# Layer norms by token tiles, a mixer that begins with dv, and the residual's affine part on VectorE

## The chip, the cores and the metric

The kernel runs on one core of a Trainium2 chip. A core has five engines with a queue each: TensorE (PE; matrix products into PSUM, and transposes), VectorE (DVE), ScalarE (ACT), GpSimd (POOL) and SyncE (SP), which issues the loads and stores. Each engine executes its own instructions in the order in which they are written; between engines, semaphores order what depends on each other. The metric is the device time of one execution in microseconds.

## The reference

One transformer block over 256 tokens of width 2048, in fp32. `ada` is a vector of shifts, scales and gates made from a condition `c`; it modulates each part, and after each part stands a layer norm over the residual:

```python
y = swiglu_ffn(x * (1 + scale[0]) + shift[0], w_ffn_in[0], w_ffn_out[0])
x = layer_norm(ALPHA * x + 0.5 * gate[0] * y, ln_g[0], ln_b[0])
y = hybrid_mixer(x * (1 + scale[1]) + shift[1], w_in, ...)
x = layer_norm(ALPHA * x + gate[1] * y, ln_g[1], ln_b[1])
y = swiglu_ffn(x * (1 + scale[2]) + shift[2], w_ffn_in[1], w_ffn_out[1])
x = layer_norm(ALPHA * x + 0.5 * gate[2] * y, ln_g[2], ln_b[2])
```

`swiglu_ffn` is `(silu(g) * u) @ w_out` with a hidden width of 5632. `hybrid_mixer` projects its input to the queries, keys and values of a differential attention (dq, dk, dv; 8 heads), to those of a gated delta rule (nq, nk, nv, with a short convolution over time, an output gate nz, and the gates nb and na), and to two merge gates (ga, gb); the two branches are merged and multiplied by `w_out`.

## The kernel before

**Precision.** Every product is made of three (`mm3`, lines 145 to 150): an operand is split into a high part of the type fp32r (ScalarE, a copy) and a low part (the operand minus its high part), and hi x hi, hi x lo and lo x hi are added up in PSUM. So each weight chunk, 128 x 1024, is loaded by SP (`raw`), split by ScalarE (`hi`) and by VectorE, or by GpSimd where `pool_lo` says so (`lo`), and then used by TensorE (`_split`, lines 177 to 198). Six `raw` buffers and four `hi`/`lo` buffers let loads and splits run ahead of the products; `weights` (line 219) hands out the next chunk of a plan that is written once for the whole kernel (lines 1524 to 1563), after issuing the splits of the next three chunks and the loads of six.

**Order.** The schedule is written out by hand. Products are emitted one after the other, and after each the kernel lets its threads (generators for the elementwise work) emit instructions when an estimated time has come. This estimate decides only the order in the queues; on the chip the engines wait for each other by semaphores.

**The two kinds of product.** `_wstat` keeps a weight tile stationary and streams 256 columns of the activations `h` (which is kept transposed, as row blocks f = 0 to 15 of 128 features by 256 tokens). `_xstat` keeps an activation tile of 128 tokens stationary and streams 512 columns of the weights; its result has tokens on the partitions. There are two token tiles, t = 0 and 1. `_y_blocks` (line 715) makes y by `_xstat` in four blocks of 512 columns and adds it to the residual `x` (`_residual`, line 700: `res` = y times the gate, the add into `x`, statistics for the layer norm). In the last block, the last two weight chunks (`TAIL`) are used tile by tile and half by half, so that t = 0 is complete first; `finish.step` (stages 0 to 3) is called at these points.

**The passage from part to part** is `_Next` (lines 549 to 629). Stage 0 sets `pool_lo` to 1 for the last block. Stage 1 (after tile 0's residual) takes tile 0's mean and variance and the root; stage 2 (after the first half of tile 1's residual) makes tile 0's factors; stage 3 (after all of it) normalises `x` (tile 0 on ScalarE, tile 1 on VectorE), and `rest` transposes `x` on TensorE into PSUM (`lnt`, 32 transposes), two row blocks with both tiles at a time, and `_h_tile` (line 516) makes of each the next part's `h`: `hf` = A times it plus B on VectorE, `h_hi` on ScalarE from `hf`, `h_lo` on GpSimd. A and B hold the layer norm's weights and the modulation. The first products (`pre`) follow as `h` becomes ready: for the mixer the keys and queries of heads 0 and 1 by `_wstat`, 192 instructions of 256 columns; for the last FFN the first block by `_xstat`, 96 of 512 columns (`wide`). In the middle of it, x is written to DRAM (`xd`) for the next residual.

**The residual's affine part.** `_load_x` (line 676) loads `x` again during a later stage, and as the stored x is normalised but not scaled, multiplies it by `ln_g` and adds `ln_b`: for each quarter of the columns and each tile two GpSimd instructions of 128 x 512, with the rows `rowg` and `rowb` in one buffer each. This happens in the mixer's merge stage and in the last FFN.

**The mixer's order** is `MIXER_JOBS` (line 41): d0, v, d1, a0, d2, a1, d3, a2, a3. A d job projects the keys and queries of two heads of the delta rule, their v, and for d0 also the gates (`_gate_proj`, `_gates`), and starts a thread for the pair (`_delta_pair`, "pair 0" and so on); v makes dv, 1024 columns in two halves; an a job makes nz and two attention heads. Group 0's keys and queries are those made in the passage.

Of the kernel before, what the change touches and what calls it, by code (L numbers as in the profile page):

```python
# [18 lines left out]
S = 256  # L19
# [72 lines left out]
class _Kernel:  # L92
# [84 lines left out]
    def _split(self):  # L177
# [14 lines left out]
        self.A.activation(hi, raw, AF.Copy)  # L192
        eng = self.P if self.pool_lo and i % self.pool_lo == 0 else self.V
        eng.tensor_tensor(lo, raw, hi.bitcast(F32), ALU.subtract)
# [92 lines left out]
def _xprod(k, ps, w, act, kt, j, t, lo, hi, last):  # L287

    act.need(k, kt)
    sl = slice(j * 512 + lo, j * 512 + hi)  # L290
    tk = slice(t * 128, (t + 1) * 128)
    k.mm3(ps[:, lo:hi], (_tile(act[0], kt)[:, tk], _tile(act[1], kt)[:, tk]), (w[0][:, sl], w[1][:, sl]),
          start=(kt == 0), stop=(kt == last))
    k.pump()
# [219 lines left out]
class _Ln:  # L514
# [25 lines left out]
    def norm(self, t, q, eng=None):  # L540
        x = self.k.x[t][:, q * 512:(q + 1) * 512]
        r, b = self.rs[:, t, 0:1], self.rs[:, t, 1:2]
        if t == 0 or eng == "A":
            self.k.A.activation(x, x, AF.Identity, bias=b, scale=r)
        else:
            self.k.V.tensor_scalar(x, x, r, b, ALU.mult, ALU.add)


class _Next:


    def __init__(self, k, idx, prep, wide):
        self.k, self.idx, self.prep, self.wide = k, idx, prep, wide

    def step(self, stage, ada, ln):
        k = self.k
        if stage == 0:
            k.pool_lo = 1
            self.A = None
        elif stage == 1:  # L560
            ln.root(0)
        elif stage == 2:
            ln.factors(0)
        else:
            ln.norm(0, 0)
            ln.norm(0, 1)
            ln.root(1)
            return self.rest(ln)
        if self.A is None and (ada.thread.done or stage == 2):
            k.wait(lambda: ada.thread.done)  # L570
            self.A, self.B = self.prep(ada)

    def rest(self, ln):
        k, A, B = self.k, self.A, self.B
        h = _new_h(k)
        x, lnp = k.x, k.lnp
        k.xd = k.drp.tile([128, 2, D], F32, tag="xd", name=f"xd{self.idx}")

        def turn(ps, g, t):
            for j in range(2):  # L580
                f = 2 * g + j
                k.tr(ps[:, j, t * 128:(t + 1) * 128], x[t][:, f * 128:(f + 1) * 128])

        def bank(g):
            ps = k.pss.tile([128, 2, 256], F32, tag="sm", name=f"lnt{k.uid()}")
            turn(ps, g, 0)
            return ps

        ln.norm(0, 2)
        ln.norm(0, 3)  # L590
        pss = [bank(g) for g in range(3)]
        ln.factors(1)
        ln.norm(1, 0)
        k.pool_lo = 0
        def run():
            for g in range(8):
                ps = pss.pop(0)
                turn(ps, g, 1)
                for i in range(2):
                    f = 2 * g + i  # L600
                    _h_tile(k, lnp, h, f, ps[:, i, :], A[:, f:f + 1], B[:, f:f + 1])
                if g in (0, 2, 4):
                    ln.norm(1, 1 + g // 2)
                h.ready = 2 * g + 2
                h.when[2 * g] = h.when[2 * g + 1] = k.chain
                yield 0.0
                if g < 5:
                    pss.append(bank(g + 3))
            for t in range(2):
                k.nc.sync.dma_start(k.xd[:, t, :], x[t])  # L610

        th = k.spawn(run())
        th.step()
        if self.wide:
            pre = [k.bank([128, 512], "pre") for _ in range(2)]
            for c in range(8):
                w = k.weights()
                for j in range(2):
                    for t in range(2):
                        _xprod(k, pre[t], w, h, 2 * c + j, j, t, 0, 512, KT - 1)  # L620
            k.wait(lambda: th.done)
            return h, pre
        acts = [h, h]
        pre = [k.bank([128, 2, S], "pre") for _ in range(2)]
        for c in range(4):
            for ps in pre:
                _products(k, ps, k.weights(), 4 * c, 4, acts, c == 0, c == 3)
        k.wait(lambda: th.done)
# [47 lines left out]
def _load_x(k, a, pool, rows, tags, idx, delay, pace):  # L676
# [11 lines left out]
    for q in range(4 if idx is not None else 0):  # L688
# [4 lines left out]
        yield 8.0  # L693
        for t in range(2):
            k.P.tensor_tensor(x[t][:, sl], x[t][:, sl], g, ALU.mult)
            k.P.tensor_tensor(x[t][:, sl], x[t][:, sl], b, ALU.add)
# [18 lines left out]
def _y_blocks(k, nchunk, act, ada, sub, first, ln, finish, tail):  # L715

    for n in range(4):
# [5 lines left out]
        def done(t, ps, lo, hi, n=n, last=last):  # L723
# [3 lines left out]
            _residual(k, n, t, ps, lo, hi, ada.dst[(sub, 2)], first, ln.st if ln else None)  # L727
# [5 lines left out]
        if last:  # L733
            k.wait(ready)
            ln.table()
            finish.step(0, ada, ln)
        _xstat(k, nchunk, act, done, tail if last else 0)
# [607 lines left out]
def _mixer(k, a, h, pre, mk_ada, finish):  # L1345
    nc, tc = k.nc, k.tc
    acts = [h, h]
    with ExitStack() as mctx:
# [5 lines left out]
        with tc.tile_pool(name="dp", bufs=1) as dp:  # L1354
# [10 lines left out]
            def delta_jobs(g):  # L1365
# [3 lines left out]
                for hd in (2 * g, 2 * g + 1):  # L1369
                    ps = _wstat(k, 4, acts) if g else pre[hd]  # L1370
                    t = dp.tile([128, 2, S], F32, tag="kq2", name=f"kq2_{hd}", bufs=4)
                    conv(t, ps, (8 + hd, hd), 1 if g else 2 - hd)
                    kq2.append(t)
                if g == 0:
                    before.append(k.spawn(_gates(k, _gate_proj(k, h))))
                ps = _wstat(k, 4, acts)
# [14 lines left out]

            for part, g in MIXER_JOBS:
# [4 lines left out]
                else:  # L1397
                    for n in range(2):
                        def done(t, ps, lo, hi, n=n):
                            yield 0.3  # L1400
                            k.A.activation(dv[:, t, n * 512:(n + 1) * 512], ps, AF.Copy)
# [363 lines left out]
```

## Time and profile before

| | us |
|---|---|
| three timed runs | 2392.42, 2395.93, 2392.65 (median 2392.65) |
| the profiled execution | 2389.68 |
| its span, from the first to the last instruction | 2387.9 |
| mean granted clock of TensorE, as a share of full speed | 0.984 |
| first passage (to the mixer) | 786.6 to 824.4 |
| mixer's jobs | to about 1270 |
| merge stage, with the residual's affine part | 1340 to 1420 |
| second passage (to the last FFN) | 1624.05 to 1659.4 |

Times in the profile are microseconds from the start of the span. TensorE's matrix products (PE) and its weight loads (PEld) have rows of their own; a busy PE can still be at half clock, which the granted clock shows. In a timeline, rows of equal instructions that follow each other are merged (x2), and the brackets hold the engine's idle time before the row and what ended it.

### The profile page before, as it was taken

To read this page: it belongs to the slowest core of one execution; us is meant where nothing else is said; L and a number is where in the kernel's file an instruction comes from. 1 tells how busy PE (TensorE), PEld (TensorE's weight loads), DVE (VectorE), ACT (ScalarE), POOL (GpSimd) and SP (SyncE) were. 2 spreads that over 40 slices of the span, in tenths; PEclk is the share of its full clock that TensorE was granted. 3 is DMA by queue.
4 is the path that set the end of the run, shared out by engine and by line. 5 is a ranking of instruction groups with operands and counts; after the bars stand their busy time and mean duration, and the time that the engine had idled before them with its cause. 6 is when DMAs were issued, how large, how long until landed. Compare 5 with 4: busy or idle time off the path is not lost.

```text
span 2387.9 us, 36796 instructions
## 1 busy us (share of the span) xinstructions
PE 2305.5 (97%) x14217; PEld 2071.9 (87%) x14217; DVE 1707.0 (71%) x2508; ACT 1033.1 (43%) x1390; POOL 329.1 (14%) x218
## 2 busy tenths in 40 slices
PE   6999999999999899999999999999999999999997
PEld 6999997888888889988999999987878888888886
DVE  5667888787775688878887887786787555544556
ACT  4434444434444444454444434444444443444432
POOL 5884000000001310000000220013050000000001
PEclk8999999999999999999999999999999999999999
DMA  9998878899875566454546888876888556655553
GB/s 362 332 327 292 300 250 274 305 339 322 315 267 189 176 204 209 157 173 149 170 162 244 298 296 306 286 282 204 310 302 309 189 192 194 193 187 192 188 187 111
DMA packets 166359, 581.70 MB, mean 244 GB/s; under 512 B 19820, under 2 KB 22812, under 8 KB 165416
## 3 DMA queue, kind: packets, MB, share of 16 engines
q1 hardware_dynamic: 166184, 579.36, 70.7%
q8 instruction: 111, 1.82, 0.3%
q14 instruction: 64, 0.52, 0.1%
HBM read 572.98 MB, written 7.88 MB: 243 GB/s over the span
## 4 chain that ended last, share of the span: by engine, by line
PE 86%; DVE 7%; issue 2%; DMA 1%; POOL 1%; ACT 1%; SPq 0%; DVEq 0%; ACTq 0%; POOLq 0%
PE mx L148 17%; PE mx L147 17%; PE mx L149 17%; PE mm L147 6%; PE mm L148 6%; PE mm L149 6%; PE mms L148 4%; PE mms L149 4%; PE mms L147 4%; DVE lo L88 2%; DVE acc L88 1%; PE UY L153 1%; DVE x L88 1%; ACT hi L88 1%; PE hT L158 1%
## 5 line engine op out<-in xcount | busy, mean ns | idle before, releaser
L88 ACT ACTIVATE hi<-raw 128x1024 fp32r<-128x1024 f32 x769 | 811.6, 1059 | 968.7 <-PE mx L149 669.3
L88 DVE TENSOR_TENSOR lo<-raw,hi 128x1024 fp32r<-128x1024 f32 x690 | 855.7, 1246 | 495.7 <-ACT hi L88 485.4
L147 PE MATMUL mx<-hi,h_hi 128*128 128x512 f32 x992 | 389.7, 393 | 0.0
L149 PE MATMUL mx<-hi,h_lo 128*128 128x512 f32 x992 | 387.2, 390 | 0.0
L148 PE MATMUL mx<-lo,h_hi 128*128 128x512 f32 x992 | 387.0, 390 | 0.0
L147 PE MATMUL mm<-h_hi,hi 128*128 128x256 f32 x1216 | 354.4, 291 | 0.0
L149 PE MATMUL mm<-h_hi,lo 128*128 128x256 f32 x1216 | 346.5, 285 | 3.4 <-DVE lo L88 3.4
L148 PE MATMUL mm<-h_lo,hi 128*128 128x256 f32 x1216 | 346.4, 285 | 0.0
L88 POOL TENSOR_TENSOR lo<-raw,hi 128x1024 fp32r<-128x1024 f32 x79 | 190.2, 2415 | 788.0 <-ACT hi L88 788.0
L147 PE MATMUL mx<-hi,hid 128*128 128x512 f32 (+1 forms) x768 | 285.1, 371 | 1.4 <-ACT hi L88 1.4
L148 PE MATMUL mx<-lo,hid 128*128 128x512 f32 (+1 forms) x768 | 284.7, 371 | 0.8 <-DVE lo L88 0.8
L149 PE MATMUL mx<-hi,hid 128*128 128x512 f32 (+1 forms) x768 | 284.5, 370 | 0.0
L147 PE MATMUL mms<-h_hi,hi 128*128 128x256 f32 x896 | 256.2, 286 | 10.2 <-ACT hi L88 5.9
L148 PE MATMUL mms<-h_lo,hi 128*128 128x256 f32 x896 | 256.2, 286 | 3.7 <-POOL h_lo L88 3.7
L149 PE MATMUL mms<-h_hi,lo 128*128 128x256 f32 x896 | 255.9, 286 | 1.6 <-POOL lo L88 1.6
L149 PEld LDWEIGHTS mm<-h_hi,lo 128*128 128x128 f32 x1216 | 235.2, 193 | 3.9 <-DVE lo L88 3.9
L147 PEld LDWEIGHTS mm<-h_hi,hi 128*128 128x128 f32 x1216 | 235.7, 194 | 1.7 <-issue 1.6
L148 PEld LDWEIGHTS mm<-h_lo,hi 128*128 128x128 f32 x1216 | 235.7, 194 | 0.7 <-issue 0.6
L149 PEld LDWEIGHTS mx<-hi,h_lo 128*128 128x128 f32 x992 | 186.6, 188 | 39.2
L147 PEld LDWEIGHTS mx<-hi,h_hi 128*128 128x128 f32 x992 | 186.7, 188 | 38.2 <-issue 0.2
L148 PEld LDWEIGHTS mx<-lo,h_hi 128*128 128x128 f32 x992 | 186.7, 188 | 38.0 <-issue 0.2
L147 PEld LDWEIGHTS mms<-h_hi,hi 128*128 128x128 f32 x896 | 174.4, 195 | 10.9 <-ACT hi L88 6.1
(304 smaller groups left out, 3236.2 us busy)
## 6 DMA issues: line engine op xcount, KB each, us to landing
raw<-in_w_ffn_in_dram SPq DMA_DIRECT2D x240, 512.0 KB, 4.7
raw<-in_w_ffn_out_dram SPq DMA_DIRECT2D x176, 512.0 KB, 4.1
raw<-in_w_first_dram SPq DMA_DIRECT2D x112, 512.0 KB, 5.0
ar<-in_w_gate_dram SPq DMA_DIRECT2D x96, 512.0 KB, 5.1
ar<-in_w_ada_dram SPq DMA_DIRECT2D x96, 512.0 KB, 5.1
sar<-in_w_ada_dram SPq DMA_DIRECT2D x64, 512.0 KB, 5.0
raw<-in_w_gab_dram SPq DMA_DIRECT2D x64, 512.0 KB, 4.5
raw<-in_w_kq_dram SPq DMA_DIRECT2D x32, 512.0 KB, 3.6
```

The source lines that it names most:

```text
L88: return f(*args, **kw)
L147: mm(ps, lhsT=lhs[0], rhs=rhs[0], start=start, stop=False, skip_group_check=True)
L148: mm(ps, lhsT=lhs[0], rhs=rhs[1], start=False, stop=False, skip_group_check=True)
L149: mm(ps, lhsT=lhs[1], rhs=rhs[0], start=False, stop=stop, skip_group_check=True)
L153: self.nc.tensor.matmul(ps, lhsT=lhsT, rhs=rhs, start=start, stop=stop, skip_group_check=True)
L158: self.nc.tensor.transpose(ps, src, self.ident if ident is None else ident)
```

## The change

- The last block of a part no longer sends the lo halves to GpSimd.
- The layer norm goes by token tile. Stage 1 makes tile 0's factors and normalises it at once, two quarters on ScalarE and two on VectorE. Stage 2 comes after tile 1's last product and before tile 1's residual: eight transposes and the first four row blocks of `h` for tile 0 alone. `h` is made in pieces of 128 x 128 (`tile`): `hf` on VectorE and `h_hi` on ScalarE both from PSUM, `h_lo` on GpSimd.
- The first products take tile 0 alone for the first four weight chunks (eight row blocks), then tile 1 for the same four, then both. In both passages they are `_xstat` products of 512 columns. Two of their chunks are split early into space that is free by then (`HELD`, `room`): the tags of hidden blocks in the first passage, in halves of 512 columns, and those of `ya` in the second.
- For the mixer these first products are the first half of dv in place of group 0's keys and queries, which now follow as in the other groups, after the gates; v makes the second half alone.
- x is written to DRAM after all first products.
- `_load_x` makes the affine part on VectorE, an instruction every 2 us by the estimate (from 8 to 12 us for a quarter).

```diff
-        self.A.activation(hi, raw, AF.Copy)
         eng = self.P if self.pool_lo and i % self.pool_lo == 0 else self.V
-        eng.tensor_tensor(lo, raw, hi.bitcast(F32), ALU.subtract)
+        parts = [(hi, lo, raw)]
+        if isinstance(hi, list):
+            parts = [(hi[j], lo[j], raw[:, j * 512:(j + 1) * 512]) for j in range(2)]
+        for h, l, r in parts:
+            self.A.activation(h, r, AF.Copy)
+            eng.tensor_tensor(l, r, h.bitcast(F32), ALU.subtract)
...
+    HELD = 2
+
+    def __init__(self, k, idx, prep):
+        self.k, self.idx, self.prep = k, idx, prep
+
+    def room(self, n):
+
+        k, j0 = self.k, SIZES[0][1] + 4 * n
+        t = [k.hp.tile([128, 512], F32R, tag=f"hid{j0 + i}", name=f"hold{k.uid()}") for i in range(4)]
+        return t[:2], t[2:]
 
     def step(self, stage, ada, ln):
         k = self.k
         if stage == 0:
-            k.pool_lo = 1
             self.A = None
         elif stage == 1:
             ln.root(0)
-        elif stage == 2:
-            ln.factors(0)
-        else:
-            ln.norm(0, 0)
-            ln.norm(0, 1)
-            ln.root(1)
-            return self.rest(ln)
         if self.A is None and (ada.thread.done or stage == 2):
             k.wait(lambda: ada.thread.done)
             self.A, self.B = self.prep(ada)
+        if stage == 1:
+            ln.factors(0)
+            for q, e in enumerate("AVVA"):
+                ln.norm(0, q, e)
+        elif stage == 2:
+            self.h = _new_h(k)
+            self.ps, self.h.ready = {}, KT
+            self.turn(0, 0)
+            self.turn(0, 1)
+            for f in range(4):
+                self.tile(0, f)
+        elif stage == 3:
+            return self.rest(ln)
+
+    def turn(self, t, g):
+
+        k = self.k
+        ps = self.ps[t, g] = k.pss.tile([128, 4, 128], F32, tag="sm", name=f"lnt{k.uid()}")
+        for j in range(4):
+            f = 4 * g + j
+            k.tr(ps[:, j, :], k.x[t][:, f * 128:(f + 1) * 128])
+
+    def tile(self, t, f):
+
+        k, h = self.k, self.h
+        src, tk = self.ps[t, f // 4][:, f % 4, :], slice(t * 128, (t + 1) * 128)
+        A, B = self.A[:, f:f + 1], self.B[:, f:f + 1]
+        hf = k.lnp.tile([128, 128], F32, tag="hf", name=f"hf{k.uid()}", bufs=4)
+        k.V.tensor_scalar(hf, src, A, B, ALU.mult, ALU.add)
+        k.A.activation(h[0][:, f, tk], src, AF.Identity, bias=B, scale=A)
+        k.P.tensor_tensor(h[1][:, f, tk], hf, h[0][:, f, tk].bitcast(F32), ALU.subtract)
 
     def rest(self, ln):
-        k, A, B = self.k, self.A, self.B
-        h = _new_h(k)
-        x, lnp = k.x, k.lnp
+        k, h = self.k, self.h
+        pre = [k.bank([128, 512], "pre") for _ in range(2)]
+
+        def products(c, w, ts):
+            for j in range(2):
+                for t in ts:
+                    _xprod(k, pre[t], w, h, 2 * c + j, j, t, 0, 512, KT - 1)
+
+        ln.root(1)
+        for f in range(4, 6):
+            self.tile(0, f)
+        ln.factors(1)
+        for q, e in enumerate("AVVA"):
+            ln.norm(1, q, e)
+        for f in range(6, 8):
+            self.tile(0, f)
+        w = [k.weights(), k.weights()]
+        products(0, w[0], (0,))
+        products(1, w[1], (0,))
+        self.turn(0, 2)
+        self.turn(0, 3)
+        w += [k.weights(), k.weights(1)]
+        products(2, w[2], (0,))
+        products(3, w[3], (0,))
+        self.turn(1, 0)
+        self.turn(1, 1)
+        for f in range(8):
+            self.tile(1, f)
+        for f in range(8, 10):
+            self.tile(0, f)
+        for c in range(4):
+            products(c, w[c], (1,))
+            if c == 1:
+                self.turn(1, 2)
+                self.turn(1, 3)
+            if c:
+                for f in (8 + 2 * c, 9 + 2 * c):
+                    self.tile(0, f)
+            if c >= 2:
+                for f in range(4 * c, 4 * c + 4):
+                    self.tile(1, f)
+        for c in range(4, 8):
+            products(c, k.weights(), (0, 1))
         k.xd = k.drp.tile([128, 2, D], F32, tag="xd", name=f"xd{self.idx}")
...
+        for t in range(2):
+            k.nc.sync.dma_start(k.xd[:, t, :], k.x[t])
...
-        yield 8.0
+        yield 4.0
         for t in range(2):
-            k.P.tensor_tensor(x[t][:, sl], x[t][:, sl], g, ALU.mult)
-            k.P.tensor_tensor(x[t][:, sl], x[t][:, sl], b, ALU.add)
+            for v, op in ((g, ALU.mult), (b, ALU.add)):
+                yield 2.0
+                k.V.tensor_tensor(x[t][:, sl], x[t][:, sl], v, op)
...
+        lead, late = last and isinstance(finish, _Next), []
+
+        def done(t, ps, lo, hi, n=n, last=last, lead=lead, late=late):
             while not ready(n):
                 yield 0.5
             yield 0.3
-            _residual(k, n, t, ps, lo, hi, ada.dst[(sub, 2)], first, ln.st if ln else None)
+
+            def residual(ps, lo, hi):
+                _residual(k, n, t, ps, lo, hi, ada.dst[(sub, 2)], first, ln.st if ln else None)
+
+            if lead and t == 1:
+                late.append((ps, lo, hi))
+                if lo:
+                    finish.step(2, ada, ln)
+                    for x in late:
+                        residual(*x)
+                return
+            residual(ps, lo, hi)
             if last and (t, lo) == (0, 256):
                 finish.step(1, ada, ln)
...
+            for i in range(finish.HELD if lead else 0):
+                k.held[k.nu + nchunk + i] = finish.room(i)
...
-                for hd in (2 * g, 2 * g + 1):
-                    ps = _wstat(k, 4, acts) if g else pre[hd]
-                    t = dp.tile([128, 2, S], F32, tag="kq2", name=f"kq2_{hd}", bufs=4)
-                    conv(t, ps, (8 + hd, hd), 1 if g else 2 - hd)
-                    kq2.append(t)
                 if g == 0:
                     before.append(k.spawn(_gates(k, _gate_proj(k, h))))
+                for hd in (2 * g, 2 * g + 1):
+                    ps = _wstat(k, 4, acts)
+                    t = dp.tile([128, 2, S], F32, tag="kq2", name=f"kq2_{hd}", bufs=4)
+                    conv(t, ps, (8 + hd, hd))
+                    kq2.append(t)
...
+            def dv_part(t, ps, n):
+                yield 0.3
+                k.A.activation(dv[:, t, n * 512:(n + 1) * 512], ps, AF.Copy)
+
+            for t in range(2):
+                k.read(dv_part(t, pre[t], 0), 2 - t)
...
+                    _xstat(k, 8, h, lambda t, ps, lo, hi: dv_part(t, ps, 1))
...
+        def room(n):
+            both = mp.tile([128, NH, S], F32R, tag=f"ya{'hl'[n]}", name=f"hold{k.uid()}").rearrange("p a b -> p (a b)")
+            return both[:, 0:1024], both[:, 1024:]
+
+        finish.room = room
         return _y_blocks(k, 8, mg, ada, 1, True, _Ln(k), finish, TAIL)
...
-                        plan += [a["w_kq"][hd, c] for c in range(4) for hd in range(2)]
+                        plan += [a["w_dv"][0, c] for c in range(8)]
                         plan += [a["w_ba"][c] for c in range(2)]
-                    else:
-                        plan += [a["w_kq"][hd, c] for hd in (2 * g, 2 * g + 1) for c in range(4)]
+                    plan += [a["w_kq"][hd, c] for hd in (2 * g, 2 * g + 1) for c in range(4)]
...
-                    plan += [a["w_dv"][n, c] for n in range(2) for c in range(8)]
+                    plan += [a["w_dv"][1, c] for c in range(8)]
```

## Rows read from the trace of the kernel before

**Rows 1.** The page's busy table: us, share of the span, instructions
```profile
PE 2305.5 (97%) x14217; PEld 2071.9 (87%) x14217; DVE 1707.0 (71%) x2508; ACT 1033.1 (43%) x1390; POOL 329.1 (14%) x218
```

**Rows 2.** Two stages, the first products alone (columns as in rows 3)
```profile
786.60:824.40 37.80, 25.91 (x192) 24.22 (x192) 0.00 (x0) 0.00 (x0) 0.91 0.50 178
...
1624.05:1659.40 35.35, 25.73 (x96) 18.49 (x96) 0.00 (x0) 0.00 (x0) 0.86 0.53 187
```

**Rows 3.** Stages: us, busy us (instructions) PE PEld DVE ACT POOL, clock, DMA
```profile
803.90:824.40 20.50, 20.50 (x173) 20.50 (x172) 11.08 (x14) 9.31 (x13) 4.61 (x7) 1.00 0.60 203
...
1641.10:1659.30 18.20, 18.19 (x82) 15.08 (x83) 11.55 (x13) 9.45 (x13) 5.99 (x9) 1.00 0.79 283
...
789.50:793.40 3.90, 2.02 (x9) 0.99 (x9) 2.80 (x9) 2.80 (x6) 0.01 (x1) 0.60 0.00 0
...
1360.00:1370.00 10.00, 10.00 (x86) 10.00 (x85) 8.92 (x8) 4.44 (x5) 6.61 (x5) 1.00 0.67 235
...
1370.00:1380.00 10.00, 7.69 (x65) 7.49 (x63) 9.93 (x8) 2.60 (x3) 7.48 (x4) 1.00 0.96 351
...
1380.00:1390.00 10.00, 8.99 (x47) 8.40 (x48) 8.93 (x9) 4.40 (x6) 6.90 (x4) 0.66 0.77 239
...
1750.00:1760.00 10.00, 8.32 (x36) 6.34 (x34) 9.93 (x8) 4.76 (x7) 6.88 (x5) 1.00 0.76 227
...
1060.00:1080.00 20.00, 16.61 (x129) 16.07 (x128) 11.66 (x32) 10.35 (x29) 2.64 (x4) 0.91 0.32 106
```

**Rows 4.** Timeline of PE: start, us, instruction, idle before and its releaser
```profile
789.48 1.37 PE L158 MATMUL lnt<-ident,x 128*128 128x128 f32 x6 [2.67 <-ACT x L88]
...
793.37 0.58 PE L147 MATMUL pre<-h_hi,hi 128*128 128x256 f32 x1 [1.08 <-ACT h_hi L88]
...
1627.52 1.54 PE L158 MATMUL lnt<-ident,x 128*128 128x128 f32 x6 [3.33 <-ACT x L88]
...
1380.72 0.79 PE L153 MATMUL aps<-acchi,ones 128*128 128x512 f32 x1 [3.03 <-ACT acchi L88]
```

**Rows 5.** Timeline of DVE in the first passage
```profile
782.98 1.97 DVE L88 TENSOR_TENSOR x<-x,res 128x256 f32<-128x256 f32 x1
...
785.76 0.42 DVE L88 TENSOR_TENSOR x<-x,res 128x256 f32<-128x256 f32 x1
...
789.86 0.37 DVE L88 BATCH_NORM_AGGREGATE mv<-st 128x2 f32<-128x48 f32 x1
...
790.99 0.55 DVE L88 TENSOR_SCALAR x<-x,rs 128x512 f32<-128x512 f32 x1
...
794.75 2.52 DVE L88 TENSOR_TENSOR lo<-raw,hi 128x1024 fp32r<-128x1024 f32 x2 [0.98 <-ACT hi L88]
```

**Rows 6.** Timeline of ACT in the first passage
```profile
788.61 1.52 ACT L88 ACTIVATE x<-x,rs 128x512 f32<-128x512 f32 x2 [1.22 <-DVE rs L88]
```

**Rows 7.** Timeline of POOL in the first passage
```profile
798.26 6.05 POOL L88 TENSOR_TENSOR h_lo<-hf,h_hi 128x256 fp32r<-128x256 f32 x8 [3.20 <-ACT h_hi L88]
```

**Rows 8.** Timeline of DVE in the merge stage
```profile
1348.52 1.85 DVE L88 TENSOR_TENSOR lo<-raw,hi 128x1024 fp32r<-128x1024 f32 x1 [0.39 <-ACT hi L88]
...
1350.29 3.48 DVE L88 SCALAR_TENSOR_TENSOR acc<-ar,cs,acc 128x512 f32<-128x512 f32 x2
...
1388.47 3.25 DVE L88 SCALAR_TENSOR_TENSOR acc<-ar,cs,acc 128x512 f32<-128x512 f32 x3
...
1393.91 1.53 DVE L88 SCALAR_TENSOR_TENSOR acc<-ar,cs,acc 128x512 f32<-128x512 f32 x2
...
1415.37 0.68 DVE L88 TENSOR_TENSOR acclo<-acc,acchi 128x512 fp32r<-128x512 f32 x1
```

**Rows 9.** Timeline of SP's queue in the merge stage
```profile
1366.09 0.33 SPq L691 DMA_DIRECT2D rowg<-in_ln_g_dram  x1
```

**Rows 10.** Chain of waits from 915 to 960: start, us, what
```profile
924.44 0.89 PE inter L153 x8
...
953.91 1.08 PE GB L153 x8
```

More of the change, by code (lines that the diff above doesn't have):

```diff
@@ L289, in _xprod @@
     act.need(k, kt)
-    sl = slice(j * 512 + lo, j * 512 + hi)
     tk = slice(t * 128, (t + 1) * 128)
-    k.mm3(ps[:, lo:hi], (_tile(act[0], kt)[:, tk], _tile(act[1], kt)[:, tk]), (w[0][:, sl], w[1][:, sl]),
+    w = [x[j][:, lo:hi] if isinstance(x, list) else x[:, j * 512 + lo:j * 512 + hi] for x in w]
+    k.mm3(ps[:, lo:hi], (_tile(act[0], kt)[:, tk], _tile(act[1], kt)[:, tk]), w,
           start=(kt == 0), stop=(kt == last))
@@ L538, in factors, with norm @@
         k.V.tensor_tensor(rs[:, t, 1:2], rs[:, t, 2:3], rs[:, t, 0:1], ALU.mult)
-    def norm(self, t, q, eng=None):
+    def norm(self, t, q, eng):
         x = self.k.x[t][:, q * 512:(q + 1) * 512]
         r, b = self.rs[:, t, 0:1], self.rs[:, t, 1:2]
-        if t == 0 or eng == "A":
+        if eng == "A":
             self.k.A.activation(x, x, AF.Identity, bias=b, scale=r)
@@ L549 @@
 class _Next:
-    def __init__(self, k, idx, prep, wide):
-        self.k, self.idx, self.prep, self.wide = k, idx, prep, wide
+    HELD = 2
[5 more added lines that the diff above has]
+        return t[:2], t[2:]
     def step(self, stage, ada, ln):
@@ L571, in step @@
             self.A, self.B = self.prep(ada)
-    def rest(self, ln):
-        k, A, B = self.k, self.A, self.B
-        h = _new_h(k)
-        x, lnp = k.x, k.lnp
-        k.xd = k.drp.tile([128, 2, D], F32, tag="xd", name=f"xd{self.idx}")
[L579 to L628, printed above, removed]
@@ L721, in ready @@
             return (sub, 2, n) in ada.ready and k.x is not None
-        def done(t, ps, lo, hi, n=n, last=last):
+        lead, late = last and isinstance(finish, _Next), []
+        def done(t, ps, lo, hi, n=n, last=last, lead=lead, late=late):
             while not ready(n):
@@ L1397, in _mixer @@
                 else:
[L1398 to L1401, printed above, removed]
-                        _xstat(k, 8, h, done)
+                    _xstat(k, 8, h, lambda t, ps, lo, hi: dv_part(t, ps, 1))
             pgs = [_wstat(k, 4, acts) for _ in range(3)]
@@ L1629, in prep1 @@
         return _affine(k, 2, 1, d[(2, 0)], d[(2, 1)])
-    h, pre = _ffn(k, a, h, 0, FFN_ADA, FFN_PACE, start, None, _Next(k, 0, prep0, False), TAIL)
-    h, pre = _mixer(k, a, h, pre, lambda pool: _Ada(k, a, pool, TAIL_ADA, TAIL_PACE), _Next(k, 1, prep1, True))
+    h, pre = _ffn(k, a, h, 0, FFN_ADA, FFN_PACE, start, None, _Next(k, 0, prep0), TAIL)
+    h, pre = _mixer(k, a, h, pre, lambda pool: _Ada(k, a, pool, TAIL_ADA, TAIL_PACE), _Next(k, 1, prep1))
     last = _Last(k, a, out)
```

## The prediction, made before the changed kernel was run

> **What bounds the kernel now.** I read the page's busy table first. TensorE is busy for 97% of the span [rows 1]: the kernel is TensorE's, and a change pays only where TensorE stands still or runs at half clock. So I went to the stages, to find where it does, and then to the timelines of the engines there. The reader is to see four places.
>
> Two are the passages between the parts, where a layer norm stands between the last product of one part and the first of the next. In the first, 786.6 to 824.4, TensorE issues 192 first products of 256 columns [rows 2] and 32 transposes. Its full rate is 173 instructions in 20.5 us, 0.1185 each [rows 3]; 192 products need 22.8 us and the transposes, at that rate, 3.8. The passage lasts 37.8: 11.2 us are lost. In the second, 1624.05 to 1659.4, 96 products of 512 columns at 18.2 / 82 = 0.222 need 21.3, the transposes 3.8, and 35.35 pass: 10.2 lost [rows 2, 3]. TensorE's own rows say where: its first transpose starts at 789.48 after 2.67 us of idling, its first product at 793.37 after a stop for `h_hi`; in the second passage it idles 3.33 us [rows 4]. VectorE's rows show what is in the way: the residuals and the statistics of both tiles come first (tile 1's norm is at 790.99), and at 794.75, after two tiles of `hf`, come two whole weight splits of 2.52 us with every later `hf` behind them [rows 5].
>
> The other two are where GpSimd makes the residual's affine part (x times ln_g plus ln_b, 16 instructions in each of two parts). From 1370 to 1390 TensorE issues 65 and 47 instructions, where it issued 86 in the ten us before, and the clock is 0.66 in the second ten: 60 fewer, 60 x 0.116 = 7.0 us. From 1750 to 1760 it issues 36 where 10 / 0.222 = 45 fit: 2.0 us [rows 3].
>
> **The change part by part.** *First passage.* I follow the new order with old durations.
> (a) In the last block the lo halves go from GpSimd to VectorE. The last one before the residuals is a split like those at 794.75 (1.26); it ends at about 783.4, where tile 0's first add started at 782.98 and, beside GpSimd's lo half, took 1.97 us instead of 0.42 [rows 5]. So the residual runs 0.9 later but 1.5 faster: tile 0's statistics are complete 0.6 earlier, at 786.05 (before: 786.65).
> (b) From aggregate to norm the old chain needs 790.99 - 789.86 = 1.13 us [rows 5]. Tile 0's norms start at 787.2 instead of 788.61; ScalarE needs 1.52 / 2 = 0.76 for one [rows 6], so the first transpose starts at 788.05 instead of 789.48. TensorE, idle from 786.64, waits 1.4.
> (c) `h` is made by token tile, 128 x 128, twice as many instructions of half the columns. GpSimd's `h_lo` of 256 columns takes 6.05 / 8 = 0.76 [rows 7]; for half I estimate 0.44, a fixed 0.1 kept. Its sum goes from 16 x 0.76 = 12.2 to 32 x 0.44 = 14.1 us. One tile's products of a row block take 3 x 0.222 = 0.67, more than 0.44, so once begun the chain feeds TensorE. The first product starts at 789.0 (before: 793.37); its two weight chunks are split already, into the room that is held, so the 2.52 us of splits leave this chain.
> (d) Row blocks 0 to 3 of tile 0 run until 791.8, and transposes 8 to 15 until 792.7. Meanwhile VectorE makes tile 1's residual, 2 x 1.35 us. Its two adds stand beside `h_lo`, as the slow add stood beside a GpSimd instruction: 0 to 2 x 1.55 us more. I take 1.2, since GpSimd is busy for under half of that time. TensorE then waits for row block 4 (1.5 us) and for 6, behind tile 1's norms (0.8).
> (e) The next two splits (chunks 4 and 5) come before tile 1's `hf`, 2.52 us on VectorE again. TensorE is on tile 0's blocks 6 and 7 and the transposes for half of it; I cost the rest at 1.3. After it GpSimd's 0.44 runs ahead of 0.67.
> Lost in the new passage: 1.4 + 0.1 + 1.5 + 0.8 + 1.3 = 5.1, and 0.8 for the switches between products and transposes: 5.9. Before, 11.2. **Gain 5.3** (bounds: 0, if each freed stop is replaced, and 9, if only the 1.4 and the switches are left).
>
> *Second passage.* The same, with four small affine instructions between the statistics and the factors (under 0.2 us each, partly beside ScalarE's root): 0.5 more, lost 6.4, before 10.2. **Gain 3.8** (0 to 8).
>
> *The write of x to DRAM* moves from the passage's middle to behind all first products. SP's queue is in order, and behind the write stand the next part's constants and gate loads, which take over x's space and wait until it is read. Raw weights are six chunks deep on that queue, 6 x 12 x 0.222 = 16 us of products, so I cost it at nothing; without that cover I bound it by a chunk's 2.7 us in each passage.
>
> *The affine part on VectorE.* 16 instructions like the 0.68 us `acclo` add 10.9 us. Off goes what GpSimd did to VectorE: an `acc` pair takes 3.48 beside it and 1.53 alone, and over the 13 slowed rows from 1348.52 to 1388.47, each against its duration in the clear, this sums to 14.6 us [rows 8]. VectorE comes out 3.7 lighter. Off goes also a block on SP: the `rowg` load of 1366.09 [rows 9] stood in the queue until GpSimd had read the previous one, with the raw loads behind it; behind a VectorE instruction of 0.68 it waits for VectorE's backlog only. The 3.03 us stop of the gate's product for `acchi` [rows 4] and the low clock behind it come from that lag. Of the 7.0 us lost I take back 4.5, as some lag stays: VectorE is busy for 8.92, 9.93 and 8.93 in those three tens [rows 3]. Bounds: 7.0, and a loss of 7.4 (were nothing to go off, 10.9 us against 2.2 free in 30, or 3.5 in the 48 that the new pace takes). In the last part, where the loss is 2.0, I take 1.5 (bounds -1 and 2). **Gain 6.0.**
>
> *The mixer begins with dv.* The mixer's products are the same in number; key and query products of group 0 (22.8 us) change places with the first half of dv (21.3). Now the gates' chain runs before the keys are done, so pair 0 of the delta rule is released by its v convolution; by the lengths of the products this is some 5 us later than before, while group 1's products come 5 us earlier: 10 us less lie between. Pair 1 starts at 953.91, 28.6 us after pair 0's products between its two tiles have ended (the eight at 924.44) [rows 10]. I cost the order at 0 (bounds: 4 us of gain from gates that are ready, 26 of loss, below).
>
> **Sum.** 5.3 + 3.8 + 6.0 = 15.1 us. The profiled execution took 2389.68 (its span 2387.9): 2374.6. The three timed runs (2392.42, 2395.93, 2392.65) have their median 2.97 above it, so the median to expect is **2377.5**.
>
> **The rivals.**
> *The clock falls all the same.* In the first passage the granted clock goes to the lower of its two levels (1.2 of 2.4 GHz) in the course of 789.5 to 793.4, mean 0.60 [rows 3], after 2.67 us of idling and some transposes; it falls in the second too. Mine begin with 1.4 us of idling, so I expect none. If it comes for as long as in the first passage (6.8 us), products that then bound the passage lose 3.4 us in each: 2384.3. For it: transposes stand at the start, as before.
> The Trainium skill, "TensorE: Matmul & The Clock Gate", Part 4 (PE-mode transpose), says that transposes do not count as TensorE being busy as products do. By that rule the 1.4 us and the transposes make one gap and the fall is likely: the 2384.3 just worked out. The rows neither bear it out nor refute it, since an idle stood ahead of the transposes both times.
>
> *The passage's stops are only exchanged.* Tile 1's residual, norms and two splits all stand on VectorE behind tile 0's `hf`; if its adds stretch to the upper bound and the splits wait for their raw loads, the passages give 4 instead of 9.1: 2382.6. Against it: the DMA share is 0.00 from 789.5 to 793.4 [rows 3], so the queue has nothing outstanding there.
>
> *VectorE stays the bound of the merge stage.* If half of the 14.6 us were time it had to spare, it gets 3.6 us heavier there, and the 4.5 vanish: 2382.0.
>
> *Slower: the delta chain falls behind.* Place: 900 to 1000, where TensorE is always busy now. Pair 0 lies 10 us nearer to group 1. It decides from the point where pair 0's chain isn't through when group 2 asks for its buffers. From 1060 to 1080 the trace shows what a stretch with late chains costs: TensorE busy for 16.61 of 20 at a clock of 0.91 [rows 3], so 3.4 us idle and 1.8 of clock. Over 100 us this is 26: 2403.5. Against it: the 28.6 us.
>
> **How the numbers follow.** My forecast with its own spread (2369 to 2382) 0.54; better than that 0.06; the clock 0.15; exchanged stops 0.09; VectorE 0.08; the delta chain 0.08. One range does, as cases with one sign hold most: 2366 to 2389 leaves out the delta chain and a tail. A measurement of this kernel can tell 0.2% (4.8 us) from no change: below 2387.9 is faster, which all but the delta chain and two mishaps together give: 0.85; within 0.09; above 2397.4 0.06.
>
> **What would show it.** The first transpose about 1.4 us after the last product and the first product 2.4 us after it (before: 6.7); no pair of `lo` between the first `hf`; first products done 31 and 31.5 us after the last product of the part before, in place of 37.8 and 35.35, at a clock of 1.00; `acc` pairs at 1.53 all through the merge stage and at least 80 TensorE instructions in each ten us there. Wrong would be: a clock of 0.5 in the new passages, TensorE waiting there for `h_lo` from GpSimd, or new stops from 880 to 1000.

## The result, and the profile after: slower, not faster

The changed kernel takes 2407.49 us (median of four, 2405.67 to 2410.5), the kernel before 2392.94 beside it: ratio 1.0059, 95% interval 1.0042 to 1.0077. 2377.5 was forecast, and 2389 was the end of the range. The profiled executions are 2410.5 (span 2408.7) and 2389.68 (span 2387.9): 20.8 us between the spans, and this is what the two traces have to explain.

The page's busy table of the changed kernel answers to [rows 1]. GpSimd is lighter, ScalarE and VectorE hardly heavier, TensorE's instructions are the same in number:

```profile
PE 2315.4 (96%) x14217; PEld 2074.2 (86%) x14217; DVE 1716.7 (71%) x2588; ACT 1047.5 (43%) x1424; POOL 241.4 (10%) x204
```

Its stages (columns as in [rows 3]): the two passages from the last product of a part to the last first product of the next; the first passage in two halves; the start of the mixer; the merge stage and the last FFN, where the residual's affine part now is on VectorE.

```profile
787.20:832.10 44.90, 32.65 (x130) 22.58 (x129) 25.98 (x57) 23.87 (x44) 14.72 (x32) 0.92 0.20 68
1631.90:1678.30 46.40, 34.40 (x132) 23.25 (x131) 26.23 (x59) 24.00 (x45) 14.70 (x32) 0.89 0.20 68
...
787.20:802.00 14.80, 11.22 (x50) 6.48 (x48) 9.64 (x25) 8.70 (x15) 3.96 (x8) 1.00 0.00 2
802.00:824.30 22.30, 14.39 (x56) 10.62 (x56) 10.46 (x27) 11.32 (x26) 10.76 (x24) 0.92 0.16 48
832.10:850.00 17.90, 12.98 (x89) 12.70 (x88) 5.69 (x9) 6.90 (x10) 0.00 (x0) 0.81 0.74 256
...
1340.00:1450.00 110.00, 110.00 (x913) 109.73 (x913) 93.41 (x118) 46.31 (x56) 0.00 (x0) 1.00 0.89 308
...
1740.00:1800.00 60.00, 60.00 (x270) 49.63 (x270) 49.78 (x59) 25.95 (x30) 0.00 (x0) 1.00 0.94 335
```

The passages last 44.9 and 46.4 us, where 37.8 and 35.35 were [rows 2] and 31.0 and 31.5 were forecast: 18.1 us longer in place of 10.7 shorter. In the first, from 802 on, TensorE is busy for 14.39 of 22.3 us. The merge stage and the last FFN are full. The mixer's start is new: TensorE stands still there and runs at a clock of 0.81.

TensorE's timeline in the first passage answers to [rows 4]. Its first rows are near the forecast (idle 1.13 before the transposes, where 1.4 was forecast; the first product 1.65 after the first transpose, where 1.0 was); then stop follows stop, for `h_hi` and for the `hi` of a weight chunk queued behind it:

```profile
788.49 1.09 PE L158 MATMUL lnt<-ident,x 128*128 128x128 f32 x8 [1.13 <-ACT x L88]
790.14 0.50 PE L147 MATMUL pre<-hold,h_hi 128*128 128x512 f32 x1 [0.56 <-ACT h_hi L88]
...
804.11 0.50 PE L147 MATMUL pre<-hold,h_hi 128*128 128x512 f32 x1 [2.24 <-ACT h_hi L88]
...
810.52 0.66 PE L158 MATMUL lnt<-ident,x 128*128 128x128 f32 x4 [1.28 <-ACT h_hi L88]
...
824.31 0.50 PE L147 MATMUL pre<-hi,h_hi 128*128 128x512 f32 x1 [3.50 <-ACT hi L88]
```

Behind these stops VectorE and ScalarE take turns, which the timelines of the two show, VectorE's first and then ScalarE's:

```profile
789.18 0.41 DVE L88 TENSOR_SCALAR hf<-lnt,affA,affB 128x128 f32<-128x128 f32 x1 [0.56 <-PE lnt L158]
790.12 0.41 DVE L88 TENSOR_SCALAR hf<-lnt,affA,affB 128x128 f32<-128x128 f32 x1 [0.53 <-ACT h_hi L88]
...
```
```profile
789.63 0.46 ACT L88 ACTIVATE h_hi<-lnt,affB,affA 128x128 fp32r<-128x128 f32 x1 [0.49 <-DVE hf L88]
790.57 0.46 ACT L88 ACTIVATE h_hi<-lnt,affB,affA 128x128 fp32r<-128x128 f32 x1 [0.48 <-DVE hf L88]
...
```

Each `h_hi` waits for its `hf`, and each `hf` for the `h_hi` of the piece before, which it does not use: what they share is the PSUM bank of four pieces that both read. A piece costs 0.94 us here and 1.01 later on. A piece that is the first of the next bank doesn't wait: the second `hf` of this row of VectorE, tile 1's fifth piece, goes right behind the fourth, and so it is at each change of bank in this stretch.

```profile
806.18 0.73 DVE L88 TENSOR_SCALAR hf<-lnt,affA,affB 128x128 f32<-128x128 f32 x2 [0.60 <-ACT h_hi L88]
```

In the kernel before, ScalarE made `h_hi` from `hf`, out of SBUF, and no `hf` waited for it. One of its rows:

```profile
797.76 1.32 ACT L88 ACTIVATE h_hi<-hf 128x256 fp32r<-128x256 f32 x3 [2.10 <-DVE hf L88]
```

The sums of the waits from 787 to 843 (us, times, longest) show these turns, and one more:

```profile
ACT h_hi L88 <- DVE hf L88: 14.2, 24, 1.8
DVE hf L88 <- ACT h_hi L88: 13.1, 22, 0.6
...
ACT dv L88 <- DMA xd<-x: 8.0, 1, 8.0
```

That one is the write of x to DRAM. The chain of waits and ScalarE's timeline have it: issued at 832.47, it takes 8.46 us. The `dv` copy, which takes over the space of x, stands at the head of ScalarE's queue until 841.51, with a weight split and `gT` behind it; TensorE's `gpn`, a product behind `gT`, then stops for 4.92 us (its row last):

```profile
832.47 0.43 SPq L655
832.90 0.05 issue
832.95 8.46 DMA xd<-x
```
```profile
841.51 1.09 ACT L88 ACTIVATE dv<-pre 128x512 f32<-128x512 f32 x2 [7.97 <-DMA xd<-x]
842.48 1.06 ACT L88 ACTIVATE hi<-raw 128x1024 fp32r<-128x1024 f32 x1
843.42 0.36 ACT L88 ACTIVATE gT<-gps 16x256 f32<-16x256 f32 x1
```
```profile
843.83 0.39 PE L158 MATMUL gpn<-ident,gT 16*128 16x16 f32 x2 [4.92 <-ACT gT L88]
```

Behind the second passage the same write (issued at 1678.36) holds up the next part's gate loads (`ar`, and `bin` behind it) on SP's queue. VectorE's `acc` waits for `bin`, a weight's lo half stands behind `acc` in its queue, and TensorE stops for that half. The waits of SP's queue and of VectorE from 1675 to 1702, and TensorE's row:

```profile
SPq L390 <- DMA xd<-x: 7.3, 1, 7.3
```
```profile
DVE acc L88 <- DMA bin<-in_b_gate_dram: 7.4, 1, 7.4
```
```profile
1697.85 0.50 PE L148 MATMUL mx<-lo,h_hi 128*128 128x512 f32 x1 [2.94 <-DVE lo L88]
```

The account of the 20.8 us. The passages make +18.1, and +1.5 because the first one's products are 1.5 us shorter than those before (21.3 and 22.8 by the prediction's rates) and the keys and queries follow later: +19.6. `gpn` adds 4.9; the low clock behind it 2.3, as the products from 844.16 to 849.01 follow each other at 0.21 us and not at 0.12. The stop at 1697.85 adds 2.9, and the low clock behind it 1.8 (eight products at 0.42 in place of 0.23, and the edges). The affine part, by the instructions that it gives back, is -11.1: 913 - 845 in the merge stage at 0.12 and 270 - 257 in the last FFN at 0.222 (the rows of before are with the second experiment). Together this is 20.4; 0.4 us I don't assign.

### The profile page after: what moved, and what is told of

Its sections match the earlier page's. It is cut to its first block, busy times and chain, and to the rows that moved or that the text cites. A ratio compares the mean times of both kernels' runs of the same rounds, so it can differ in the third digit from the quotient of the medians.

```text
span 2408.7 us, 36902 instructions
## 1 busy us (share of the span) xinstructions
PE 2315.4 (96%) x14217; PEld 2074.2 (86%) x14217; DVE 1716.7 (71%) x2588; ACT 1047.5 (43%) x1424; POOL 241.4 (10%) x204
## 4 chain that ended last, share of the span: by engine, by line
PE 85%; DVE 7%; ACT 3%; DMA 2%; issue 1%; POOL 0%; SPq 0%; DVEq 0%; ACTq 0%; POOLq 0%
PE mx L148 16%; PE mx L149 16%; PE mx L147 16%; PE mm L147 7%; PE mm L148 7%; PE mm L149 7%; PE mms L148 4%; PE mms L149 4%; PE mms L147 4%; DVE lo L88 2%; ACT h_hi L88 1%; ACT hi L88 1%; DVE hf L88 1%; DMA xd<-x 1%; PE UY L153 1%
## 5 line engine op out<-in xcount | busy, mean ns | idle before, releaser
L148 PE MATMUL mx<-lo,h_hi 128*128 128x512 f32 x960 | 374.5, 390 | 2.9 <-DVE lo L88 2.9
L147 PE MATMUL mx<-hi,h_hi 128*128 128x512 f32 x960 | 376.7, 392 | 0.0
L149 PE MATMUL mx<-hi,h_lo 128*128 128x512 f32 x960 | 374.7, 390 | 0.0
L147 PE MATMUL mm<-h_hi,hi 128*128 128x256 f32 x1280 | 374.2, 292 | 0.0
L149 PE MATMUL mm<-h_hi,lo 128*128 128x256 f32 x1280 | 365.5, 286 | 0.6 <-DVE lo L88 0.5
L148 PE MATMUL mm<-h_lo,hi 128*128 128x256 f32 x1280 | 365.4, 285 | 0.0
L147 PEld LDWEIGHTS mm<-h_hi,hi 128*128 128x128 f32 x1280 | 249.0, 195 | 2.3 <-issue 2.1
L148 PEld LDWEIGHTS mm<-h_lo,hi 128*128 128x128 f32 x1280 | 249.1, 195 | 1.0 <-issue 0.7
L149 PEld LDWEIGHTS mm<-h_hi,lo 128*128 128x128 f32 x1280 | 248.6, 194 | 1.0 <-DVE lo L88 1.0
L148 PEld LDWEIGHTS mms<-h_lo,hi 128*128 128x128 f32 x896 | 174.5, 195 | 4.3 <-POOL h_lo L88 4.2
```

What stands on the lines that cost most here:

```text
L147: mm(ps, lhsT=lhs[0], rhs=rhs[0], start=start, stop=False, skip_group_check=True)
L148: mm(ps, lhsT=lhs[0], rhs=rhs[1], start=False, stop=False, skip_group_check=True)
L149: mm(ps, lhsT=lhs[1], rhs=rhs[0], start=False, stop=stop, skip_group_check=True)
```

## The experiments

Theory A: the passages are long because the two readers of one PSUM bank go one after the other. Its rival: small pieces simply cost about 1 us. Theory C: the late write of x makes the stops behind the passages. Each of the two sets of four ran on one chip with the kernel before: 2395.45 us for the first set, 2394.51 for the second.

**ScalarE reads `hf`.** The changed kernel, with this edit in `tile`:

```
-        k.A.activation(h[0][:, f, tk], src, AF.Identity, bias=B, scale=A)
+        k.A.activation(h[0][:, f, tk], hf, AF.Copy)
```

> The changed kernel with one line different: ScalarE makes h_hi from hf in SBUF (a copy, as before the change) and no longer from the transposes in PSUM. Theory (turns at the bank): in the changed kernel hf on VectorE and h_hi on ScalarE read the same PSUM bank and take turns, 32 pieces of about 1.0 us a passage. Then here hf follows hf at 0.3 to 0.4 us, the first products end 35 to 37 us after the last product instead of 45 and 46, and the time falls by 16 to 20 us to 2388 to 2392. Rival (small pieces): the fixed costs of twice as many instructions make the chain long, whoever reads what; the instructions here are as many and as small, so the passages stay at 45 and 46 us and the time at 2405 to 2408.

Measured 2378.36 us, ratio 0.9927 (0.9912 to 0.9942): more than was expected. The passages fall to 31.3 us each and not to 35 to 37: the 3.50 us stop for a split queued behind `h_hi` is gone too, and the longest stop left is 1.71. The pieces are as small as before, but `hf` no longer waits for `h_hi`: of those 13.1 us nothing is left. By lines, from 787 to 820 (busy, mean ns, idle before):

```profile
L88 DVE TENSOR_SCALAR hf<-lnt,affA,affB 128x128 f32<-128x128 f32 x32 | 12.3, 406 | 0.7 <-PE lnt L158 0.6
L88 ACT ACTIVATE h_hi<-hf 128x128 fp32r<-128x128 f32 x32 | 9.9, 311 | 4.5 <-DVE hf L88 2.3
```

The rival falls. But the edit changes two things, the bank and ScalarE's instruction (311 ns in place of 456); a later run keeps the instruction.

**The affine part alone**, on VectorE, in the kernel before:

```
-            k.P.tensor_tensor(x[t][:, sl], x[t][:, sl], g, ALU.mult)
-            k.P.tensor_tensor(x[t][:, sl], x[t][:, sl], b, ALU.add)
+            for v, op in ((g, ALU.mult), (b, ALU.add)):
+                yield 2.0
+                k.V.tensor_tensor(x[t][:, sl], x[t][:, sl], v, op)
```

> The kernel before with only the residual's affine part moved to VectorE (with the new pace). If the merge stage after the change shows this part's own worth (no ten us below 83 instructions of TensorE from 1360 to 1450), the time falls by 7 to 10 us to 2383 to 2386: 7 from the merge stage, 2 from the last FFN. Rival (the added 10.9 us of VectorE are a cost that other parts of the change cover): 2391 to 2397.

Measured 2380.78, ratio 0.9939 (0.9924 to 0.9954): 14.7 us won, not 7 to 10. Stages of the kernel before, and then two of this one (the third is full as well, 270 instructions):

```profile
1360.00:1400.00 40.00, 36.69 (x278) 35.89 (x277) 36.80 (x32) 15.29 (x18) 20.99 (x12) 0.91 0.79 271
1400.00:1450.00 50.00, 48.74 (x402) 48.18 (x401) 42.02 (x51) 20.38 (x25) 0.00 (x0) 1.00 0.90 317
1740.00:1800.00 60.00, 57.80 (x257) 47.14 (x256) 52.89 (x48) 25.91 (x31) 29.96 (x16) 1.00 0.86 309
...
1340.00:1450.00 110.00, 105.43 (x845) 104.07 (x844) 96.58 (x99) 42.83 (x51) 29.71 (x16) 0.97 0.85 295
```
```profile
1360.00:1400.00 40.00, 40.00 (x334) 39.91 (x334) 35.50 (x46) 15.43 (x18) 0.00 (x0) 1.00 0.89 301
1400.00:1450.00 50.00, 50.00 (x417) 49.91 (x416) 44.08 (x55) 22.43 (x27) 0.00 (x0) 1.00 0.88 306
```

VectorE does 14 and 4 instructions more in about the time it was busy before, and TensorE never stops. The loss reached past 1390, where I had stopped counting: 56 + 15 instructions at 0.12 are 8.5 us, and 2.9 come in the last FFN. These 11.4 are less than the 14.7 between the medians, and the two profiled spans (2387.9 and 2378.9) lie only 9.0 apart: the profiled execution of before was one of the shorter ones, and where the others lose the rest, its trace can't show.

**x written early.** The changed kernel, in `rest`: the write goes out right behind tile 1's norms, before its first products.

```
         for q, e in enumerate("AVVA"):
             ln.norm(1, q, e)
+        k.xd = k.drp.tile([128, 2, D], F32, tag="xd", name=f"xd{self.idx}")
+        for t in range(2):
+            k.nc.sync.dma_start(k.xd[:, t, :], k.x[t])
```

> The changed kernel with the write of x issued right after tile 1's norms instead of behind all first products. Theory (the write holds space): ScalarE's dv copies no longer wait 8 us for it, TensorE's 4.9 us stop at 843 goes with the low clock behind it (3.4 us), and so does the 2.9 us stop at 1698: 8 to 11 us less, 2396 to 2400. Rival (the space is late anyway, by the constants' loads or by SP's queue): under 3 us less. By the turns theory the passages themselves stay at 45 and 46 us.

Measured 2397.82 (2395.77 to 2399.55, ten runs), ratio 1.0013 (1.0003 to 1.0022), as expected. The stops of `gpn` and at 1697.85 are gone; the turns remain, as theory A wants:

```profile
ACT h_hi L88 <- DVE hf L88: 14.2, 24, 1.8
DVE hf L88 <- ACT h_hi L88: 13.2, 22, 0.6
```

**Both edits.**

> The changed kernel with both: h_hi from hf, and the write of x issued early. If the two causes are separate and together the whole of the loss, the gains add up: 16 to 20 and 8 to 11, 2377 to 2383, which is what the prediction of 2377.5 was for the change without these two. Rival (small pieces): no better than with the early write alone, 2396 to 2400.

Measured 2369.16 (2364.73 to 2370.25), ratio 0.9886 (0.9871 to 0.9901): the early write is worth 9.2 us on top of the first edit. This is 8 us below the expected range, as the first edit alone had won more than was expected. The two passages now last 31.2 and 31.4 us at full clock, where 31.0 and 31.5 had been forecast, and the stops left in the first are short. By the stages, and then all five on TensorE's timeline:

```profile
787.40:818.60 31.20, 26.94 (x130) 21.15 (x130) 26.24 (x57) 20.06 (x44) 13.79 (x32) 1.00 0.41 157
1611.50:1642.90 31.40, 27.02 (x130) 21.25 (x130) 26.25 (x57) 20.05 (x44) 14.22 (x33) 1.00 0.42 159
```
```profile
788.57 1.09 PE L158 MATMUL lnt<-ident,x 128*128 128x128 f32 x8 [1.13 <-ACT x L88]
790.07 0.50 PE L147 MATMUL pre<-hold,h_hi 128*128 128x512 f32 x1 [0.41 <-ACT h_hi L88]
...
794.44 0.50 PE L147 MATMUL pre<-hi,h_hi 128*128 128x512 f32 x1 [0.39 <-ACT h_hi L88]
...
796.80 0.50 PE L147 MATMUL pre<-hi,h_hi 128*128 128x512 f32 x1 [0.61 <-ACT h_hi L88]
...
801.12 0.50 PE L147 MATMUL pre<-hold,h_hi 128*128 128x512 f32 x1 [1.72 <-ACT h_hi L88]
```

**Two banks.** The changed kernel with nothing moved but the pieces' places: a turn's eight pieces go alternately into its two banks. The instructions on VectorE, ScalarE and GpSimd, their shapes and their order stay.

```
-            f = 4 * g + j
+            f = 8 * (g // 2) + 2 * j + g % 2
...
-        src, tk = self.ps[t, f // 4][:, f % 4, :], slice(t * 128, (t + 1) * 128)
+        src, tk = self.ps[t, 2 * (f // 8) + f % 2][:, f % 8 // 2, :], slice(t * 128, (t + 1) * 128)
```

> The changed kernel with one edit: the eight transposed pieces of a turn are laid in turn into two PSUM banks, even pieces into one, odd ones into the other, in place of four after four. Every instruction, its engine, its shape and its order on VectorE, ScalarE and GpSimd stay; only the bank that a piece lies in changes. Theory A (the two readers of one bank go one after the other): VectorE can now read the next piece while ScalarE reads this one, so a piece costs one instruction, 0.41 to 0.5 us, in place of 0.94 to 1.01; the waits of hf for h_hi vanish, the passages fall to about 32 us, and the time comes to 2376 to 2384, as with h_hi made from SBUF. The rival (two engines that read PSUM get in each other's way whatever the bank, or small pieces cost 1 us per pair by themselves): the period stays at about 1 us and the time at 2404 to 2411.

Measured 2381.84, ratio 0.9955 (0.9939 to 0.9972), as theory A wants; the passages last 32.1 and 32.2 us, and of the 13.1 us that `hf` waited for `h_hi` 1.6 are left. Four pieces now go through without a gap, 0.45 us each (VectorE's and ScalarE's timelines):

```profile
788.14 1.79 DVE L88 TENSOR_SCALAR hf<-lnt,affA,affB 128x128 f32<-128x128 f32 x4 [0.56 <-PE lnt L158]
```
```profile
788.59 1.83 ACT L88 ACTIVATE h_hi<-lnt,affB,affA 128x128 fp32r<-128x128 f32 x4 [0.49 <-DVE hf L88]
```

The two engines do read PSUM side by side, from two banks. This bears theory A out: it is the bank, not PSUM and not the piece. Two things stay open. Each of these banks holds one tile of the program, so no run tells whether the order goes by the bank or by the tile. And the profile has the wait of `hf` as one for a semaphore of `h_hi`, an order that was laid into the program; what the two reads would do to each other without it, no run shows.

**Two banks and x early.**

> The two banks and x written to DRAM right after the norms of tile 1. If the two faults of the changed kernel are independent, the second is worth here the 10 us that it was worth with the bank left as it was (2407.5 to 2397.8) and with h_hi from SBUF (2378.4 to 2369.2): 2366 to 2374, within 4 us of the version with h_hi from SBUF. If reading PSUM twice costs more than reading SBUF once, it lies above that version by the difference of the pieces (32 x 0.05 us a passage, some 3 us in all).

Measured 2369.06 (2367.88 to 2369.89), ratio 0.9894 (0.988 to 0.9909), as expected. The two cures of the turns are worth the same, and both versions beat the changed kernel and the kernel before.

**The affine part back on GpSimd**, with both edits: the second experiment's diff taken back.

> h_hi from SBUF and x written early, but the residual's affine part back on GpSimd in its old pace: what the passages and the mixer's order are worth alone. By the sums of the passages (37.8 to 31.2 us and 35.35 to 31.7) 10 us under the kernel before if the mixer's order costs nothing: 2382 to 2386 where the kernel before takes 2393 to 2395. By the difference that the affine part alone made (profiled spans 2387.9 and 2378.9) it lies 9 us above the version with everything, 2377 to 2381. The rival (the parts lean on each other: the affine part's stops lie ahead of the second passage and shift it): less than 6 us under the kernel before, 2387 or more.

Measured 2383.16, ratio 0.9952 (0.9937 to 0.9967): the passages and the mixer's order are worth 11.4 us under the kernel before. The passages are 6.6 and 3.95 us shorter (31.2 and 31.4 here too), but 1.5 of that are the shorter products of the first one, for which the mixer takes as much longer later: 9.05 won, where 9.1 was forecast. The order costs nothing that can be seen. Its stages show GpSimd's affine part in the way again (44, 26 and 24 instructions fewer than in the full rows above):

```profile
1360.00:1400.00 40.00, 36.78 (x290) 36.22 (x290) 37.02 (x34) 12.88 (x15) 16.52 (x10) 0.96 0.79 286
1400.00:1450.00 50.00, 47.90 (x391) 47.04 (x391) 42.25 (x51) 23.13 (x28) 0.00 (x0) 1.00 0.88 306
1740.00:1800.00 60.00, 56.84 (x246) 46.09 (x245) 49.77 (x45) 25.27 (x30) 24.73 (x14) 0.97 0.88 314
```

**Splits later**, a try at the 1.72 us stop: the splits of chunks 4 and 5 behind tile 1's sixth piece and behind tile 0's tenth (`look(n)` issues the splits that `weights` would).

```
-        w = [k.weights(), k.weights()]
+        w = [k.weights(1), k.weights(1)]
...
-        w += [k.weights(), k.weights(1)]
+        w += [k.weights(2), k.weights(3)]
...
+        for f in range(6):
+            self.tile(1, f)
+        look(1)
...
+        look(2)
```

> The version with h_hi from SBUF and x written early, in which the splits of chunks 4 and 5 are called behind six and ten more pieces of h, not ahead of all of tile 1's. The longest stop left in each passage, 1.72 us at the first product of tile 1 for h_hi behind 2.36 us of lo halves on VectorE, should go: 3 us less than that version, 2363 to 2367. The rival: the stop moves to the first product of chunk 4, whose lo half is then late by about as much: no difference (within 1 us), with a PE stop of 1 to 2 us for hi or lo some 8 us later.

Measured 2373.87 (2373.07 to 2374.72), ratio 0.9915 (0.99 to 0.993), 4.7 us above the version that it starts from (the intervals of the two ratios just meet): neither the gain nor the rival's equal time. The passages are longer, 33.6 and 33.7 us. The stop fell to 0.48, but others came (TensorE's timeline and then VectorE's): VectorE now idles 2.36 us for the transposes, in which it had made the lo halves, and waits for ScalarE at each split:

```profile
804.82 0.66 PE L158 MATMUL lnt<-ident,x 128*128 128x128 f32 x4 [1.03 <-DVE hf L88]
...
809.99 0.50 PE L147 MATMUL pre<-hi,h_hi 128*128 128x512 f32 x1 [1.10 <-ACT h_hi L88]
```
```profile
799.41 2.16 DVE L88 TENSOR_SCALAR hf<-lnt,affA,affB 128x128 f32<-128x128 f32 x6 [2.36 <-PE lnt L158]
802.90 1.23 DVE L88 TENSOR_TENSOR lo<-raw,hi 128x1024 fp32r<-128x1024 f32 x1 [1.33 <-ACT hi L88]
```

## Why the prediction was wrong

**Step (c) failed.** "One tile's products of a row block take 3 x 0.222 = 0.67, more than 0.44, so once begun the chain feeds TensorE": this took GpSimd's `h_lo` for the slowest link of a chain whose links overlap. The 0.44 was right (0.46 measured). But the edit also moved ScalarE's source from `hf` to the transposed piece in PSUM, and I costed the piece's size alone. Two readers of one bank made the link 0.41 + 0.46 and the hand-overs, 0.94 to 1.01 us, more than 0.67. The 32 pieces of the first passage take 27.6 us this way (20.1 of it for the last 24, from 803.17 to 823.31), and with tile 1's residual, its norms and two splits between them they became the passage's length. Undone, it gives back 25 to 32 us (the ratio from 1.0059 to 0.9955 and to 0.9927).

The Trainium skill, "PSUM — Partial Sum Buffer", section "PSUM bank collisions raise a hardware error", says that two engines must not touch one bank and quadrant at once, reads against reads included, and that the compiler's scheduler puts a dependency between any two such instructions, ScalarE and VectorE too. The traces agree: the turns are there with one bank (0.94 us a piece) and gone with two (0.45). By that rule this stop could have been told from the diff.

**The write of x failed too.** "I cost it at nothing; without that cover I bound it by a chunk's 2.7 us in each passage." I looked for who would wait on SP's queue and took the cover of raw weights. In the first passage the waiter is another: ScalarE, whose `dv` copy takes over x's space, and with it a split and the gates. In the second it is VectorE, whose `acc` waits for a load held up behind the write, with a lo half behind it. The price is 8.0 us of ScalarE and 4.9 of TensorE in the first, 2.9 in the second, and low clock behind both: 9 to 13 us in all (9.2, 9.7 and 12.8 between the three pairs of runs with and without).

**The affine part: right in direction, mis-sized.** 6.0 forecast, bounds to 9.0; 14.7 measured alone and 14.0 between the two versions that differ in nothing else (2383.16 and 2369.16, each from its own set of runs; 15.8 by their ratios). I took back 4.5 of 7.0 in the merge stage "as some lag stays", and none stayed; my bound came from 30 us of that stage, and it loses 15 more instructions from 1400 to 1450; and the profiled execution of before was a mild one, 2389.68 against a median of 2395.45 in the first set: in the run with the affine part back, the same three stretches lose 44 + 26 instructions at 0.12 and 24 at 0.222, 13.7 us.

**The rest held.** Steps (a) and (b): idle 1.13 against 1.4, first product 2.8 us after the last one against 2.4. Steps (d) and (e) and the second passage, once the turns are out: 31.2 and 31.4 us against 31.0 and 31.5. In the sum, that is: the stops of (d) were 0.39 and 0.61, where 1.5 and 0.8 were forecast, and that of (e) 1.72, where 1.3 was. The mixer's order: no cost to be seen, and TensorE in the changed kernel busy 119.25 of 120 us from 880 to 1000, so the delta chain did not fall behind. Of the rivals, the clock did not fall at the passage's head: 1.13 us of idling and eight transposes stand there, and the granted clock is 1.00 from 787.2 to 802. The passages' means of 0.92 and 0.89 come from further on, behind the stops; without these it is 1.00 through both passages. So the rule on transposes that the prediction weighed (the Trainium skill, "TensorE: Matmul & The Clock Gate", Part 4) decides nothing here: the fall that the prediction took from it didn't come. "The passage's stops are only exchanged" came nearest, by another mechanism and at more than five times its price (28.8 us above the forecast of the two passages, where it had 5.1). Of the prediction's signs of being wrong the low clock came, for some us behind the stops; what made the stops, TensorE waiting for ScalarE's `h_hi`, none of them named.

So two unseen waits cost 25 to 32 and 9 to 13 us, against a change that without them wins 25 to 26 (2369 of 2394.5 to 2395.5), more than the 15.1 forecast, and that mostly by the affine part.

## What to carry to other kernels

When an edit gives two engines the same PSUM tile to read, add their durations, not the larger one: let the second read the first's copy in SBUF, or lay consecutive pieces into different banks. When a transfer out of a buffer moves back, look for everything that takes over that buffer's space, on every engine, and for who waits for the loads behind it on its queue. And read an operand's source in the diff as closely as its shape: both cost.

## What was not expected of the hardware

ScalarE's small piece is no cheaper from PSUM than its larger one was from SBUF: 456 ns for 128 columns out of PSUM, 311 for the same out of SBUF, 418 for 256 out of SBUF in the kernel before. The one out of PSUM also applies a scale and a bias where the others copy, and the runs don't tell the two apart. And VectorE took over 16 instructions of 0.68 us in the merge stage and was no busier for it: 93.41 us of 110, against 96.58 with GpSimd beside it, as an `acc` took 749 ns on average and not 912 (a pair 1.53 and up to 3.48 [rows 8]).
